# Hybrid trunk on one NeuronCore: the first feed-forward layer in a written order, with the state-space table operations on the vector engine

## The chip, the cores and the metric

The kernel runs on one core of one Trainium2 chip. The time is device microseconds of that core, and the time before is the median of three runs.

## The reference, cut to what matters

A two-layer decoder trunk over 512 positions of 1024 channels. Each layer has a mixer (layer 0: stick-breaking attention beside causal pooling; layer 1: a state-space layer), then a cross-attention into 256 memory tokens, then a gated feed-forward layer. The two parts that the change touches are the feed-forward layer and the constants of the state-space layer:

```python
def conv_gated_mlp(h, w_up, conv_w, conv_b, w_down):     # D_FF = 2816
    up = h @ w_up                                        # 512 x 5632
    padded = jnp.pad(up, ((0, 0), (CONV_WIDTH - 1, 0), (0, 0)))
    conv = conv_b
    for i in range(CONV_WIDTH):                          # 3 taps, causal
        conv = conv + conv_w[i] * padded[:, i:i + seq]
    val, gate = jnp.split(conv, 2, axis=-1)
    return (jax.nn.silu(gate) * val) @ w_down
...
    # s5_ssm: 64 groups of 16 channels, 64 complex states per group
    bb_re = coef_re[..., None] * b_re - coef_im[..., None] * b_im
    bb_im = coef_re[..., None] * b_im + coef_im[..., None] * b_re
    # h_t = Lbar h_{t-1} + Bbar u_t ;  y = Re(C h) + D u
```

The kernel computes the state-space layer in blocks of 8 positions. For that it needs, per group, products of B and of C with powers of Lbar, and a small table of taps made from both. These tables depend on the weights alone. They are made during the first feed-forward layer, written to DRAM, and read back in the state-space layer.

## The kernel before

Everything is held transposed: `xT[m]` are 8 tiles of 128 channels x 512 positions. A projection of 1024 inputs to 128 outputs is 8 steps of `mm3`, and each `mm3` is three matmuls of 512 columns (high x high, high x low, low x high), because every operand is split into two reduced-precision parts. A weight chunk (four 128x128 blocks, 256 KB) is loaded on SP's queue into `wr`, copied by ScalarE to `wh` (L112) and subtracted by VectorE to `wl` (L115). There are four buffers of each, so a chunk can be converted three chunks before the matmuls use it.

The feed-forward layer has 22 hidden blocks in two halves of 11. In a half, each block has an up-projection of the value (`up_conv(j)`) and of the gate (`up_conv(NF + j)`), 24 matmuls each, and then the convolution: a multiply by the norm row on VectorE (L1311), ScalarE's tap (L1313), two taps on VectorE (L1314, L1316). The gate goes through SiLU (L1329), is multiplied (L1330) and split into `hh` and `hl`. Then come 8 down-projections `psd` of 33 matmuls each, added to `xT` by `residual`. This layer appears twice: layer 0 (`ffn` with `side`), and layer 1 with the same work and no side work, to which the first can be compared.

The side work of layer 0 is the generator `ssm_prep`. For 16 blocks of B it forms two products and a sum on GpSimd (L597 to L599, 128x512), which TensorE transposes (`pswi`), ScalarE copies out (L607) and SP writes to `d_win`. For 16 blocks of C it does the same with 9 powers (L643 to L645, 128x576). The result, laid out `[4, 16, 9]`, is copied by ScalarE (L649) and written to `d_wout`; TensorE multiplies it with the B table (`psk`, L654); the taps are copied (L657), get the skip term from two small VectorE operations (L659, L661), are spread by eight small DMAs on SP's queue into `tz` (L665), reordered by ScalarE (L667) and written to `d_t`. All of these transfers are on SP's queue, which also carries every weight chunk.

Most stages of this kernel are under `tc.manual_schedule()`, which keeps the order in which the program is written on each engine. The region of the first feed-forward layer is not: there the framework's planner orders the instructions by its own costs and may move them forward across the region's start. The PSUM banks of that region are split by use (A=2, B=4, C=2). Weight chunks for the two feed-forward layers come from a list of their own (`wcols`, one column block ahead, L123), those of the other stages from one stream `W` (L167), which `take()` keeps three raw chunks and four converted chunks ahead.

The stage before is the first cross-attention, which ends with eight output projections `pso`. GpSimd makes another set of tables there (`ssm_tables`, `d_tab`). The stage behind is the state-space layer. It reads the tables back with GpSimd's queue (`load_x`, `load_y`) and starts with the projections `psu`, then the first use of a table (`psX`, L1513).

Of the kernel before, what the change touches and what calls it, by code (L numbers as in the profile page):

```python
# [52 lines left out]
def trunk_kernel(  # L53
# [21 lines left out]

    pools = {}
# [473 lines left out]
    def ssm_prep(rg):  # L550
        yield
        pB, pBi = (rg.tile([128, 8, 64], F32, tag=f"pw{q}", name="pB") for q in range(2))
        pC, pCi = (rg.tile([128, 9, 64], F32, tag=f"pw{2 + q}", name="pC") for q in range(2))
        for q, t in enumerate((pB, pBi, pC[:, 1:9], pCi[:, 1:9])):
            nc.sync.dma_start(out=t.rearrange("p a b -> p (a b)"), in_=d_pw[q])
# [4 lines left out]
        def raw_pair(src, order, c_major):  # L560
# [4 lines left out]
            d1 = rg.tile([128, 16, 64], F32, tag="rw1", name="rw1")  # L565
            d2 = rg.tile([128, 16, 64], F32, tag="rw2", name="rw2")
            for c0 in (0, 8):
# [4 lines left out]
                o1 = d1[:, c0:c0 + 8, :].rearrange("p a b -> p (a b)")  # L572
                o2 = d2[:, c0:c0 + 8, :].rearrange("p a b -> p (a b)")
                A.activation(out=o1, in_=ps, func=AF.Copy)
                A.activation(out=o2[0:64], in_=ps[64:128], func=AF.Copy)
                A.activation(out=o2[64:128], in_=ps[0:64], func=AF.Copy)
            return d1, d2

        b1, b2 = raw_pair((ssm_b_re[0], ssm_b_im[0]),
                          "g (r p c) -> g r p c", False)  # L580
        yield
        bz = rg.tile([128, 64, 16], F32, tag="bz", name="bz")
        LAG = 4
        pend = []
        for b in range(2 * NB):
            gs = slice(b * 4, b * 4 + 4)
            sh = [128, 4, 16, 8]
            big = rg.tile([128, 4, 16, 8], F32, tag="u2", bufs=9, name="bl")
            bt = rg.tile([128, 4, 16, 8], F32, tag="u2", bufs=9, name="bt")
# [12 lines left out]
            def fin(b=b, big=big):  # L602
                ps = psC("pswi")
                for q in range(4):
                    tr(ps[:, q * 128:(q + 1) * 128], big[:, q].rearrange("p c j -> p (c j)"))
                w = rg.tile([128, 512], F32, tag="ev", bufs=2, name="wi")
                A.activation(out=w, in_=ps, func=AF.Copy)  # L607
                nc.sync.dma_start(out=d_win[b // 2][:, (b % 2) * 512:(b % 2) * 512 + 512], in_=w)

            pend.append(fin)  # L610
            if len(pend) > LAG:
                pend.pop(0)()
            yield

        while pend:
            pend.pop(0)()
            yield
        c1, c2 = raw_pair((ssm_c_re[0], ssm_c_im[0]),
                          "g (c r p) -> g c r p", True)

        dsk = rg.tile([64, 16], F32, tag="dsk", name="dsk")
        nc.sync.dma_start(out=dsk, in_=ssm_d[0].rearrange("(g c) -> g c", c=16))
# [5 lines left out]
        for t in tzs:  # L628
            G.memset(t, 0.0)
# [1081 lines left out]
```

## Time and profile before

| what | value |
|---|---|
| time, median of 3 runs | 1553.75 us (1552.21 to 1555.38) |
| profiled execution, on the device | 1556.48 us |
| its span, first to last instruction | 1554.7 us |
| mean granted TensorE clock | 0.987 |

The profiled execution has 1.8 us around its span and is 2.7 us over the median of the runs. In the rows below, a line such as L115 is a line of the kernel before; a tile name such as `psup` is the program's. PE is TensorE, DVE VectorE, ACT ScalarE, POOL GpSimd, SP the engine that issues most DMAs. A name ending in q is an engine's queue of instructions that are not counted as busy.

### The profile page before, as it was taken

To read this page: it belongs to the slowest core of one execution; us is meant where nothing else is said; L and a number is where in the kernel's file an instruction comes from. 1 tells how busy PE (TensorE), PEld (TensorE's weight loads), DVE (VectorE), ACT (ScalarE), POOL (GpSimd) and SP (SyncE) were. 2 spreads that over 40 slices of the span, in tenths; PEclk is the share of its full clock that TensorE was granted. 3 is DMA by queue.
4 is the path that set the end of the run, shared out by engine and by line. 5 is a ranking of instruction groups with operands and counts; after the bars stand their busy time and mean duration, and the time that the engine had idled before them with its cause. 6 is when DMAs were issued, how large, how long until landed. Compare 5 with 4: busy or idle time off the path is not lost.

```text
span 1554.7 us, 21034 instructions
## 1 busy us (share of the span) xinstructions
PE 1509.6 (97%) x7327; PEld 1238.7 (80%) x7327; DVE 1024.5 (66%) x1523; ACT 727.5 (47%) x1286; POOL 482.2 (31%) x739
## 2 busy tenths in 40 slices
PE   8999999998988999999999999999999999999998
PEld 6787988887866887777778897888888888888887
DVE  4776656665799866887655667455656775367754
ACT  5556664343434542455553546433444443244532
POOL 7775339995399058330000111000000000000002
PEclk9999899999999999999999999999999999999999
DMA  6213234324323533345464877333123333333331
GB/s 193 78 44 105 82 124 124 99 82 136 89 81 95 154 106 108 107 148 181 142 212 139 267 227 243 110 102 89 55 70 101 95 96 92 97 101 96 95 116 54
DMA packets 282613, 183.99 MB, mean 118 GB/s; under 512 B 30279, under 2 KB 260235, under 8 KB 282507
## 3 DMA queue, kind: packets, MB, share of 16 engines
q1 hardware_dynamic: 264011, 149.84, 32.6%
q0 software_dynamic: 7264, 25.20, 4.7%
q10 hardware_dynamic: 11232, 7.61, 1.6%
q8 instruction: 57, 0.93, 0.2%
q14 instruction: 49, 0.40, 0.1%
HBM read 156.13 MB, written 24.12 MB: 116 GB/s over the span
## 4 chain that ended last, share of the span: by engine, by line
PE 70%; POOL 11%; DVE 7%; issue 5%; DMA 3%; ACT 3%; SPq 0%; DVEq 0%; ACTq 0%; POOLq 0%
PE psup L206 8%; PE psup L208 8%; PE psup L207 8%; PE psd L206 5%; PE psd L208 5%; PE psd L207 5%; DVE wl L115 2%; PE psg L206 2%; PE psg L207 2%; PE psg L208 2%; PE pso L207 2%; PE pso L208 2%; PE pso L206 1%; PE psk L654 1%; POOL tb L541 1%
## 5 line engine op out<-in xcount | busy, mean ns | idle before, releaser
L115 DVE TENSOR_TENSOR wl<-wr,wh 128x512 fp32r<-128x512 f32 (+2 forms) x467 | 361.0, 782 | 137.0 <-ACT wh L112 134.7
L112 ACT ACTIVATE wh<-wr 128x512 fp32r<-128x512 f32 (+2 forms) x467 | 283.5, 618 | 318.3 <-PE psd L207 108.3
L208 PE MATMUL psup<-xh,wl 128*128 128x512 f32 x704 | 277.8, 395 | 11.6 <-DVE wl L115 11.6
L206 PE MATMUL psup<-xh,wh 128*128 128x512 f32 x704 | 279.9, 398 | 1.4 <-ACT wh L112 1.4
L207 PE MATMUL psup<-xl,wh 128*128 128x512 f32 x704 | 277.2, 394 | 0.0
L1383 POOL TENSOR_TENSOR acc<-acc,sq 128x256 f32<-128x256 f32 x12 | 8.8, 734 | 559.1 <-ACT sq L1381 558.9
L208 PEld LDWEIGHTS psup<-xh,wl 128*128 128x128 f32 x704 | 133.4, 190 | 44.7 <-DVE wl L115 16.1
L206 PEld LDWEIGHTS psup<-xh,wh 128*128 128x128 f32 x704 | 133.4, 190 | 34.7 <-ACT wh L112 3.5
L207 PEld LDWEIGHTS psup<-xl,wh 128*128 128x128 f32 x704 | 133.5, 190 | 27.5 <-issue 0.5
L206 PE MATMUL psd<-hh,wh 128*128 128x512 f32 x328 | 129.7, 395 | 0.0
L208 PE MATMUL psd<-hh,wl 128*128 128x512 f32 x328 | 129.1, 394 | 0.0
L207 PE MATMUL psd<-hl,wh 128*128 128x512 f32 x328 | 129.0, 393 | 0.0
L1313 ACT ACTIVATE fc<-fu,ccols 128x512 f32<-128x512 f32 x88 | 71.8, 816 | 103.1 <-DVE fu L1311 103.1
L1314 DVE SCALAR_TENSOR_TENSOR fc<-fu,ccols,fc 128x511 f32<-128x511 f32 x88 | 71.7, 814 | 24.0 <-ACT fc L1313 24.0
L1311 DVE TENSOR_TENSOR fu<-psup,rbc 128x512 f32<-128x512 f32 x88 | 60.3, 685 | 40.2 <-PE psup L208 37.6
L1316 DVE SCALAR_TENSOR_TENSOR fc<-fu,ccols,fc 128x510 f32<-128x510 f32 x88 | 75.3, 856 | 2.9
L206 PEld LDWEIGHTS psd<-hh,wh 128*128 128x128 f32 x328 | 61.6, 188 | 16.3 <-issue 1.3
L208 PEld LDWEIGHTS psd<-hh,wl 128*128 128x128 f32 x328 | 61.6, 188 | 14.3
L207 PEld LDWEIGHTS psd<-hl,wh 128*128 128x128 f32 x328 | 61.6, 188 | 14.0
L301 ACT ACTIVATE xh<-xT,gcols 128x512 fp32r<-128x512 f32 x40 | 33.5, 838 | 83.3 <-DVE xT L324 55.0
L206 PE MATMUL pso<-oh,wh 128*128 128x512 f32 x128 | 51.1, 399 | 4.9 <-ACT wh L112 4.9
L115 DVE TENSOR_TENSOR hl<-fc,hh 128x512 fp32r<-128x512 f32 x44 | 37.3, 847 | 25.8 <-ACT hh L112 25.6
(331 smaller groups left out, 3388.0 us busy)
## 6 DMA issues: line engine op xcount, KB each, us to landing
wr<-in_ffn_w_up_dram SPq DMA_DIRECT2D x176, 256.0 KB, 2.9
wr<-in_ffn_w_down_dram SPq DMA_DIRECT2D x70, 256.0 KB, 2.9
wr<-in_xa_w_kv_dram SPq DMA_DIRECT2D x64, 256.0 KB, 3.3
wr<-in_ab_w_in_dram SPq DMA_DIRECT2D x32, 256.0 KB, 2.9
wr<-in_xa_w_q_dram SPq DMA_DIRECT2D x32, 256.0 KB, 2.8
wr<-in_xa_w_o_dram SPq DMA_DIRECT2D x32, 256.0 KB, 2.8
wr<-in_ssm_w_glu_dram SPq DMA_DIRECT2D x29, 256.0 KB, 2.7
wr<-in_ffn_w_down_dram SPq DMA_DIRECT2D x24, 192.0 KB, 2.6
```

The lines of the kernel that those rows point to most:

```text
L112: A.activation(out=o, in_=i, func=AF.Copy)
L115: V.tensor_tensor(out=o, in0=i, in1=hi.bitcast(F32), op=ALU.subtract)
L206: T.matmul(ps, lhsT=lh, rhs=rh, start=first, stop=False)
L207: T.matmul(ps, lhsT=lh, rhs=rl, start=False, stop=False)
L208: T.matmul(ps, lhsT=ll, rhs=rh, start=False, stop=last)
L301: A.activation(out=ho, in_=src, func=AF.Copy, scale=g)
L541: G.tensor_tensor(out=dst[0], in0=dst[0], in1=tq[:, :, :c], op=ALU.subtract)
L654: T.matmul(ps[0:16, q * 128:(q + 1) * 128], lhsT=bz[:, b * 4 + q, :], rhs=big[:, q, :, 0:8].rearrange("p c m -> p m c"), start=True, stop= ...
L1311: V.tensor_tensor(out=u, in0=ps, in1=rbc, op=ALU.mult)
L1313: A.activation(out=c, in_=u, func=AF.Identity, scale=cwcol(layer, 2, t), bias=cbcol(layer, t))
L1314: V.scalar_tensor_tensor(out=c[:, 1:], in0=u[:, :511], scalar=cwcol(layer, 1, t), in1=c[:, 1:], op0=ALU.mult, op1=ALU.add)
L1316: V.scalar_tensor_tensor(out=c[:, 2:], in0=u[:, :510], scalar=cwcol(layer, 0, t), in1=c[:, 2:], op0=ALU.mult, op1=ALU.add)
```

## The change

The first feed-forward layer gets a function of its own, `ffn_side`, under `manual_schedule` and with all eight PSUM banks in one pool. Its weights come from the stream `W`, whose list now runs unbroken from the cross-attention through this layer and the state-space layer. The gate product and its split are written one convolution later. The generator of the side work is stepped by hand: once in each convolution, and in the down-projections 2, 2 and 1 times behind the chunks of the first half and once behind each chunk of the second. A step issues one table operation, and what follows from it is issued a fixed number of steps later (`at(n, f)`).

The products and sums of the tables move from GpSimd to VectorE. The C table is laid out `[4, 9, 16]`, so `psk` reads 128 contiguous columns, while ScalarE's copy of it is now the one with a stride. The two small tap operations move from VectorE to GpSimd, and the copy of B's last power to ScalarE. All loads and stores of the side work move from SP's queue to GpSimd's. At the start of the kernel eight matmuls on a tile of ones are added and the first value step is split in two.

```diff
+    np_.tile([128, 32], F32, tag="pad", name="pad")
...
-                nc.sync.dma_start(out=rv[:, :, q, :] if c_major else rv[:, q], in_=src[q])
+                nc.gpsimd.dma_start(out=rv[:, :, q, :] if c_major else rv[:, q], in_=src[q])
...
-            G.tensor_tensor(out=big, in0=vb(b1), in1=vp(pB), op=ALU.mult)
-            G.tensor_tensor(out=bt, in0=vb(b2), in1=vp(pBi), op=ALU.mult)
-            G.tensor_tensor(out=big, in0=big, in1=bt, op=ALU.add)
-            G.tensor_copy(bz[:, gs, :], big[:, :, :, 7])
+            V.tensor_tensor(out=big, in0=vb(b1), in1=vp(pB), op=ALU.mult)
+            yield
+            V.tensor_tensor(out=bt, in0=vb(b2), in1=vp(pBi), op=ALU.mult)
+            yield
+            V.tensor_tensor(out=big, in0=big, in1=bt, op=ALU.add)
...
+            at(2, turn)
+            at(3, keep)
+            at(4, put)
...
-            sh = [128, 4, 16, 9]
+            sh = [128, 4, 9, 16]
...
-                    T.matmul(ps[0:16, q * 128:(q + 1) * 128], lhsT=bz[:, b * 4 + q, :],
-                             rhs=big[:, q, :, 0:8].rearrange("p c m -> p m c"), start=True, stop=True)
+                    T.matmul(st["ps"][0:16, q * 128:(q + 1) * 128], lhsT=bz[:, b * 4 + q, :],
+                             rhs=big[:, q, 0:8, :], start=True, stop=True)
...
-                V.tensor_tensor(out=kt[:, :, 0, :], in0=kt[:, :, 0, :], in1=dd, op=ALU.add)
+                G.tensor_tensor(out=kt[:, :, 0, :], in0=kt[:, :, 0, :], in1=dd, op=ALU.add)
...
-                    nc.sync.dma_start(out=tz[j:128:8, :, j * 16:128], in_=ktf[:, :, 0:128 - j * 16])
+                    nc.gpsimd.dma_start(out=tzs[b % 2][j:128:8, :, j * 16:128], in_=ktf[:, :, 0:128 - j * 16])
...
+            for n, f in ((1, wout), (2, taps), (2, put_wout), (3, keep), (3, spread), (8, band), (9, put_band)):
+                at(n, f)
...
+    ffn_weights(0)
+    ssm_weights()
+    xattn_weights(1)
...
+        warm = psC("warm")
+        for _ in range(8):
+            T.matmul(warm[:, 0:128], lhsT=ones, rhs=ones, start=True, stop=True)
         W.cap[0] = 1
         x_tile(0)
         W.fill()
+        v_step(0, range(2))
         x_tile(1)
         W.cap[0] = 2
         W.fill()
-        v_step(0)
+        v_step(0, range(2, 4))
...
+    def ffn_side(rg, layer, norm, hid_extra, nxt, side):
+        acts = norm.acts
+        SIDE = ((2, 2, 1), (1, 1, 1))
+        st = {"n": 0}
+        wait = {}
+        def conv(t, ps):
+            u = rg.tile([128, 512], F32, tag="fu", bufs=2, name="fu")
+            V.tensor_tensor(out=u, in0=ps, in1=st["rbc"], op=ALU.mult)
+            c = rg.tile([128, 512], F32, tag="fc", bufs=3, name="fc")
+            A.activation(out=c, in_=u, func=AF.Identity, scale=cwcol(layer, 2, t), bias=cbcol(layer, t))
+            gate = wait.pop("gate", None)
+            if gate:
+                cv, cg, hl = gate
+                V.tensor_tensor(out=cv, in0=cv, in1=cg, op=ALU.mult)
+                copy_hi(hl[0], cv)
+            next(side, None)
+            V.scalar_tensor_tensor(out=c[:, 1:], in0=u[:, :511], scalar=cwcol(layer, 1, t), in1=c[:, 1:],
+                                   op0=ALU.mult, op1=ALU.add)
+            V.scalar_tensor_tensor(out=c[:, 2:], in0=u[:, :510], scalar=cwcol(layer, 0, t), in1=c[:, 2:],
+                                   op0=ALU.mult, op1=ALU.add)
+            if gate:
+                sub_lo(hl[1], cv, hl[0])
+            return c
...
+                for n in SIDE[hf]:
+                    hi, lo = W.take()
...
+                    for q in range(hi.shape[1]):
+                        mm3(ps, hi[:, q, :], lo[:, q, :], hid[k][0], hid[k][1], k == 0, k == NH - 1)
+                        k += 1
+                    for _ in range(n):
+                        next(side, None)
+                residual(m, ps)
...
-    with banks(A=2, B=4, C=2), region("rgB") as rg:
+    with banks(X=8), region("rgB") as rg, tc.manual_schedule():
         side = ssm_prep(rg)
-        ffn(rg, 0, n_f0, 4, n_mix1, side)
+        next(side)
+        ffn_side(rg, 0, n_f0, 4, n_mix1, side)
```

## Rows read from the trace of the kernel before

**Rows 1.** Page, part 1: busy time, share of the span, instructions.

```profile
PE 1509.6 (97%) x7327; PEld 1238.7 (80%) x7327; DVE 1024.5 (66%) x1523; ACT 727.5 (47%) x1286; POOL 482.2 (31%) x739
```

**Rows 2.** Windows: stretch, length, busy time of PE, PEld, DVE, ACT, POOL; clock; DMA.

```profile
380.00:396.15 16.15, 16.10 (x60) 13.06 (x61) 11.03 (x17) 7.82 (x13) 0.00 (x0) 0.84 0.48 137
396.15:549.46 153.31, 140.94 (x615) 111.30 (x614) 132.28 (x143) 67.33 (x111) 93.65 (x64) 0.96 0.36 105
549.46:616.67 67.21, 67.11 (x303) 52.27 (x301) 42.49 (x43) 23.64 (x40) 54.80 (x31) 1.00 0.35 104
616.67:761.29 144.62, 144.04 (x617) 107.00 (x616) 109.18 (x151) 76.02 (x119) 30.71 (x23) 1.00 0.48 144
761.29:828.22 66.93, 66.93 (x290) 51.91 (x290) 34.68 (x51) 34.88 (x50) 3.73 (x7) 1.00 0.60 189
828.22:853.63 25.41, 25.41 (x124) 20.94 (x122) 15.43 (x35) 9.89 (x18) 1.82 (x2) 1.00 0.42 127
1177.15:1298.86 121.71, 121.71 (x540) 100.29 (x539) 90.20 (x143) 59.34 (x90) 0.00 (x0) 1.00 0.32 94
1298.86:1360.45 61.59, 61.59 (x266) 49.55 (x264) 23.26 (x36) 16.52 (x28) 0.00 (x0) 1.00 0.33 97
1360.45:1480.14 119.69, 119.69 (x529) 99.10 (x528) 87.57 (x129) 57.45 (x87) 0.00 (x0) 1.00 0.34 99
```

**Rows 3.** Waits, 416 to 549.46 us: total us, times, longest.

```profile
PE psup L208 <- DVE wl L115: 11.0, 8, 2.1
```

**Rows 4.** Groups by line, DVE, 416 to 549.46 us: busy, mean ns | idle before.

```profile
L115 DVE TENSOR_TENSOR wl<-wr,wh 128x512 fp32r<-128x512 f32 x38 | 44.5, 1171 | 0.3 <-ACT wh L112 0.3
```

**Rows 5.** Groups by line, DVE, 1360.45 to 1480.14 us (the second feed-forward layer).

```profile
L115 DVE TENSOR_TENSOR wl<-wr,wh 128x512 fp32r<-128x512 f32 x44 | 30.2, 686 | 2.1 <-ACT wh L112 1.9
```

**Rows 6.** Groups by line, POOL, whole span.

```profile
L598 POOL TENSOR_TENSOR bt<-rw,pB 128x512 f32<-128x512 f32 x16 | 30.2, 1884 | 0.0
```

**Rows 7.** Waits of SP's queue, 270 to 860 us.

```profile
SPq L564 <- DMA d_tab<-tb: 17.5, 1, 17.5
```

**Rows 8.** Timeline of SP, 373 to 376 us: start, length, instruction.

```profile
375.33 1.07 SPq L167 DMA_DIRECT2D wr<-in_xa_w_o_dram  x2
```

**Rows 9.** Timeline of PE at 380 us; in brackets the idle time before and its releaser.

```profile
380.05 0.80 PE L206 MATMUL pso<-oh,wh 128*128 128x512 f32 x1 [4.92 <-ACT wh L112]
```

**Rows 10.** Timeline of PE, 597 to 600 us: one group of tap matmuls.

```profile
597.29 2.00 PE L654 MATMUL psk<-dl,bz 128*16 128x128 f32 x8
599.22 0.50 PE L206 MATMUL psd<-hh,wh 128*128 128x512 f32 x1
```

**Rows 11.** Timeline of PE, 549.4 to 550.2 us: one group of transposes.

```profile
549.46 0.60 PE L216 MATMUL pswi<-cs,bl 128*128 128x128 f32 x4
549.82 0.48 PE L206 MATMUL psd<-hh,wh 128*128 128x512 f32 x1
```

**Rows 12.** Groups by line, DVE, whole span: an operand read with a 32-byte stride.

```profile
L1639 DVE TENSOR_TENSOR xT<-xT,sig 128x512 f32<-128x512 f32 x8 | 9.3, 1168 | 0.2
```

**Rows 13.** Instructions of L548: issue time on POOL, ns min/median/max, first and last start.

```profile
L548 POOL DMA_DIRECT2D d_tab<-tb x16: 551/568/667, 243.7 to 370.5; - x16
```

**Rows 14.** Instructions of tile tz: issue time on SP; then from issue to landing.

```profile
L665 SPq DMA_DIRECT2D tz<-kt x128: 544/593/1493, 600.6 to 799.0; - x128
...
DMA to landing us min/median/max: 1.7/1.9/8.6
```

**Rows 15.** Timeline of POOL, 600 to 850 us: table reads of the state-space layer.

```profile
788.05 0.54 POOL L1490 DMA_DIRECT2D wo<-d_wout  x1 [1.78 <-ACT wo L649]
844.99 0.92 POOL L1505 DMA_DIRECT2D sg<-d_u  x1 [56.40 <-DMA d_u<-su]
```

**Rows 16.** DMA issues by line: count, KB each, median us to landing.

```profile
wo<-d_wout POOLq DMA_DIRECT2D x8, 512.0 KB, 7.3
```

**Rows 17.** Timeline of DVE, 12 to 13 us: the second converted weight chunk.

```profile
12.22 0.69 DVE L115 TENSOR_TENSOR wl<-wr,wh 128x512 fp32r<-128x512 f32 x1 [1.69 <-ACT wh L112]
```

**Rows 18.** Timeline of PE, 12 to 14.2 us: the first matmul that uses that chunk.

```profile
13.91 0.48 PE L206 MATMUL psv<-wh,xh 128*128 128x512 f32 x1
```

More of the change, by code (lines that the diff above doesn't have):

```diff
@@ L610, in ssm_prep @@
-            pend.append(fin)
-            if len(pend) > LAG:
-                pend.pop(0)()
-            yield
[L615 to L622, printed above, removed]
-        ps = psC("psds")
-        tr(ps[0:16, 0:64], dsk, 64)
-        dcol = rg.tile([16, 64], F32, tag="dcol", name="dcol")
@@ L1286, in xattn, with ffn @@
             nxt.tile(m)
-    def ffn(rg, layer, norm, hid_extra, nxt, side=None, tail=0):
+    def ffn(rg, layer, norm, hid_extra, tail):
         acts = norm.acts
@@ L1325, in ffn @@
                 cv = up_conv(j)
-                if pace[0] != "slow":
-                    pace[0] = next(side, None)
                 cg = up_conv(NF + j)
@@ L1339, in ffn @@
                 sub_lo(hl[1], cv, hl[0])
-                pace[0] = next(side, None)
                 hid.append(hl)
@@ L1354, in ffn, with up @@
                     late.append(hl)
-                pace[0] = next(side, None)
                 residual(m, ps)
-                if hf == 1 and not tail:
+        finish(hid[NH - tail:], late)
+    def ffn_side(rg, layer, norm, hid_extra, nxt, side):
[21 more added lines that the diff above has]
+            return c
+        def up(t):
+            ps = psB("psup")
+            sproj(ps, acts)
+            if "rc" not in st:
+                st["rc"] = norm.stats_cols()
+                st["first"] = ps
+                return None
+            if "rbc" not in st:
+                st["rbc"] = norm_row(st["rc"], 4)
+            return ps
+        for hf in range(2):
+            hid = []
+            for j in range(hf * NH, (hf + 1) * NH):
+                ps = up(j)
+                cv = conv(j, ps) if ps is not None else None
+                ps = up(NF + j)
+                if cv is None:
+                    cv = conv(j, st.pop("first"))
+                cg = conv(NF + j, ps)
+                A.activation(out=cg, in_=cg, func=AF.Silu)
+                hl = []
+                for nm in ("hh", "hl"):
+                    if st["n"] % 12 < hid_extra:
+                        hl.append(rg.tile([128, 512], F32R, tag="hx", bufs=2 * hid_extra, name=nm))
+                    else:
+                        hl.append(ttile(nm))
+                st["n"] += 1
+                hid.append(hl)
+                wait["gate"] = (cv, cg, hl)
+            for m in range(KD):
+                ps = psA("psd")
+                k = 0
+                for n in SIDE[hf]:
+                    hi, lo = W.take()
+                    gate = wait.pop("gate", None)
+                    if gate:
+                        cv, cg, hl = gate
+                        V.tensor_tensor(out=cv, in0=cv, in1=cg, op=ALU.mult)
+                        copy_hi(hl[0], cv)
+                        sub_lo(hl[1], cv, hl[0])
+                    for q in range(hi.shape[1]):
[4 more added lines that the diff above has]
+                residual(m, ps)
+                if hf == 1:
```

212 lines of the change are left out of this document (127 added, 85 removed).

## The prediction

> **What bounds the kernel now.** The page's busy times come first. TensorE is busy for 97% of the span, VectorE for 66%, ScalarE for 47% and GpSimd for 31% [rows 1]. So time can only be won where TensorE waits, where it runs at half clock, or where it does something that it need not. Busy time alone shows none of the three, because a stretched matmul counts as busy.
>
> The second view is the windows, one for each half and part of the two feed-forward layers [rows 2]. The second layer does the same 1584 matmuls of projection without side work, so its stretches are the measure: 121.71 us for the first 22 up tiles, 119.69 for the other 22, 61.59 for eight down tiles. Its last down part has another form, so 61.59 stands for both. The sum is 121.71 + 61.59 + 119.69 + 61.59 = 364.6 us. The first layer takes 153.31 + 67.21 + 144.62 + 66.93 = 432.1 us. The excess is 67.5 us.
>
> Next, what fills that excess. The side work's own matmuls are seen in the timeline. A group of eight tap matmuls takes 599.22 - 597.29 = 1.93 us [rows 10], and there are 16 groups, 30.9 us. A group of four transposes `pswi` takes 549.82 - 549.46 = 0.36 us [rows 11], 16 groups are 5.8 us. The other side transposes (`psrw`, `psds`), 33 in number, are some 3 us at the same 0.09 each. That is 39.7 us, and 67.5 - 39.7 = 27.8 us remain that are no work at all.
>
> Most of the 27.8 us lies in the first up part: 153.31 - 121.71 - 6.8 (15 groups `pswi` and 16 of the other transposes) = 24.8. There VectorE is busy 132.28 of 153.31 us, and GpSimd 93.65 [rows 2]. The waits name the link: matmuls of `psup` stand waiting for `wl`, the low half of a weight chunk from VectorE, 11.0 us in 8 waits [rows 3], and the clock of the stretch is 0.96 [rows 2]. The groups by line show why `wl` is late: it takes 1171 ns here [rows 4] and 686 ns in the second layer [rows 5]. The difference between the two stretches is that GpSimd's table operations, 1884 ns each [rows 6], run beside VectorE's in the first. In the other parts VectorE has less to do and the slower operations stay hidden.
>
> Last, the cross-attention's end. SP's queue holds the side work's first load (L564), moved forward by the planner, and it waits 17.5 us for `d_tab` [rows 7]. The next weights stand behind it and are issued at 375.33 [rows 8]. [...]
>
> **The change part by part.**
>
> *Table products off GpSimd.* With them goes what slows VectorE. I take the 27.8 us of lost time in the first layer as gone, provided that VectorE can carry the work itself. That is 96 operations in 96 steps, 64 products and 32 sums. A sum is contiguous, 0.69 us [rows 5], and 0.77 for 576 columns in proportion. A product reads one operand with a stride of 256 bytes. The trace has no such operation on VectorE; below, it can't be cheaper than contiguous, 0.69; the nearest row above is an operand at 32 bytes, 1.17 [rows 12]; the far bound is GpSimd's 1.88 [rows 6]. I take 1.17, and 1.3 for 576 columns, since stride is what the row has in common. A step is then 1.01 us (B) or 1.12 (C) on average.
>
> An up part takes 22 steps, 22 to 25 us, on top of 87.57 to 90.20: 112 of some 126 us. The first down part takes 40 steps (8 tiles x 5), 42 us, on top of 23.26: 65 us. TensorE's side there is 61.59 + 10 x 0.36 and about two tap groups, 66 to 67 us. The second takes 16 table operations, 18 us, and the eight norm tiles of some 1.9 us (one strided, one contiguous operation), so 23.26 + 18 + 15 = 56 of 66 us. So VectorE stays below TensorE everywhere, closest in the first down part. Being late by a few us there is covered: conversion runs three chunks ahead, and a chunk of 12 matmuls is 12 x 119.69/528 = 2.7 us, so 8 us of cover. Term: -27.8 us; the bounds are -27.8 and, with products at 1.88, -17 (below).
>
> *The tap matmuls read contiguous columns.* Now 128 columns take 1.93/8 = 0.241 us each, with the elements 36 bytes apart. In the same kernel, 128 contiguous columns of a transpose take 0.36/4 = 0.09 [rows 11], and a 512-column matmul 0.227, so 0.057 for 128. If stride is not the reason, 0.241 stays. I take 0.09, the row of the same width and type: 128 x (0.241 - 0.09) = -19.3 us, with bounds 0 and 128 x (0.241 - 0.057) = -23.6. [...]
>
> *Side transfers off SP's queue.* The load that blocked weights now waits on GpSimd's queue, behind the same `d_tab` stores, where only the table work waits for it; its first use is the third step, behind two up tiles. So the 4.92 us go, and with them the slow clock, 16.15 x 0.16 = 2.6 us. Term: -7.5 us; bound 0, if another load is late there.
>
> On GpSimd a DMA issue takes 0.57 us [rows 13], against SP's 0.59 for `tz` [rows 14]. A C block issues two stores and eight small DMAs and has two operations of 64 columns, which I put at 0.45 each, twice an eighth of [rows 6]'s 1.88: some 6.6 us of GpSimd. Blocks come every 16 us in the up part, every 5 in the first down part (three blocks), every 7.5 in the second. The chain that matters is the single buffer `kt`: ScalarE copies taps, then 0.9 + 8 x 0.57 + 1.9 to landing [rows 14] = 7.4 us until it may copy again. In the first down part ScalarE stands for some 2 us once; behind it the next weight conversions wait, and the 8 us of cover hold. At nothing, then, and at the price of the rival below if the chain is longer.
>
> *What moves to a later point.* Before, the state-space layer's first table reads were issued during the feed-forward layer, the tenth at 788.05 [rows 15], 40 us before the layer began. Now GpSimd's queue keeps program order, and all ten (512 KB each) are issued in the first 10 x 0.54 = 5.4 us of that layer, behind the last `put_band`. Each lands in 7.3 us [rows 16]. The first two are wanted with `psX` 25.4 us after the start, which covers them. What is late next is `sg(0)`, issued 16.8 us after the start (844.99 - 828.22) [rows 15], behind them in the same queue. It has 25.41 - 16.8 = 8.6 us until `psX` and needs some 7.3, so it fits if its own source, written in the same traffic, isn't late. Bounds 0 and +8 us (one more landing); I take +2.
>
> *At nothing:* the eight matmuls on ones run while TensorE waits for the first input; the split value step only moves matmuls before the second chunk, which is ready at 12.91 [rows 17], and first used at 13.91 [rows 18], so up to 1 us either way. ScalarE's strided copies: it has half of its time free [rows 2]. The late gate product has a whole convolution before its first use.
>
> Sum: -27.8 - 19.3 - 7.5 + 2 = -52.6 us. For the profiled execution, 1556.48 - 52.6 = 1503.9 (span 1554.7 plus 1.8); it was 2.7 over the median, so against the median 1553.75 - 52.6 = 1501.
>
> **The rivals.**
>
> *VectorE becomes the bound.* If a stride of 256 bytes costs 1.88 per product, the first down part has 23.26 + 27 x 1.88 + 13 x 0.7 = 83 us of VectorE against 66, 17 us late, of which the cover of conversions ahead takes some 6: 11 us. Elsewhere it still fits. 1501 + 11 = 1512. For it: no row has that stride. Against: stride costs the same 2 ns for an element on VectorE (1.17/512) and TensorE (0.241/128 = 1.9).
>
> *The layout is not why the taps are slow.* They stay at 0.241, and the time is 1501 + 19 = 1520. For it: their weights are only 16 columns wide, which no other row has.
>
> *The state-space layer waits for its tables.* The reads and `sg(0)` land 8 to 12 us late: about 1510. For it: ten reads, weights and `d_u` at once. Against: the projections hold more than 25 us.
>
> *The spread of the taps on GpSimd's queue becomes the pace, and the kernel is slower.* ScalarE stands still for every block whose chain is longer than the distance of blocks. Some 7.6 blocks are at 7 us, the rest at 16. From a chain of 7 + 53/7.6 = 14 us the whole gain is gone; at 16 us it is 7.6 x 9 = 68 us, 1569 us. [...] Against: the stores of `d_tab` took 0.67 us at most beside a working VectorE [rows 13], and the eight need not land one after another.
>
> **How the numbers follow.** The forecast has 0.62, VectorE as the bound 0.10, slow taps 0.08, late tables 0.12, the slow chain 0.04; 0.04 is left for what I don't see. The forecast's own range is 1495 (taps at 0.057, no wait at the tables, 4 + 2 us) to 1509. 1494 to 1522 holds the first four but for their edges, and I go to 1492 and 1523 for the 1.6 us by which the runs shown lie around their median. A change of 0.2%, 3 us, is what a measurement of this kernel tells from none. Faster by more: 0.94. Within: 0.02. Slower: 0.04.
>
> **What would show it.** In the changed profile the first feed-forward layer takes about 385 us, with parts near 127, 67, 128 and 64. `wl` has a mean near 0.69 throughout. A group of eight tap matmuls takes 0.7 us. TensorE's idle time at the cross-attention's end is gone. Products on VectorE are near 1.17 and 1.3 us. GpSimd's reads are issued at the state-space layer's start, and `psX` follows some 25 to 28 us after it. The prediction is wrong if ScalarE is seen waiting for `tz`'s DMAs by many us at a time, or if `wl` stays late with GpSimd idle.

## The result and the profile after

| what | before | after |
|---|---|---|
| median of 4 runs each, side by side | 1552.98 us (1551.05 to 1555.38) | 1514.44 us (1513.06 to 1515.88) |
| ratio, with its 95% interval | | 0.9751 [0.9733, 0.9769] |
| profiled execution | 1556.48 us | 1513.59 us |
| its span | 1554.7 us | 1511.8 us |

The change makes the kernel 38.5 us faster. The forecast was 52.6 us faster, 1501 us. The two profiled spans differ by 42.9 us, because the profiled execution of before lay 3.5 us above the median beside it and that of after 0.9 below: the shares below are of the 42.9.

The windows of the kernel after, by stage: the four parts of the first feed-forward layer, the head of the state-space layer in two pieces, and three parts of the second feed-forward layer. Columns as in [rows 2].

```profile
387.45:515.83 128.38, 128.38 (x593) 105.04 (x591) 102.26 (x160) 64.79 (x110) 3.90 (x6) 1.00 0.36 102
515.83:586.56 70.73, 68.24 (x325) 54.95 (x324) 58.86 (x77) 27.72 (x55) 12.77 (x26) 1.00 0.46 141
586.56:715.71 129.15, 129.15 (x594) 103.94 (x592) 107.37 (x153) 70.63 (x108) 47.20 (x94) 1.00 0.43 127
715.71:783.72 68.01, 68.01 (x313) 53.45 (x313) 50.80 (x66) 46.28 (x63) 41.44 (x85) 1.00 0.51 159
783.72:810.21 26.49, 25.58 (x124) 20.80 (x122) 12.61 (x29) 8.31 (x15) 6.91 (x15) 1.00 1.00 344
810.21:830.00 19.79, 16.30 (x89) 14.75 (x90) 14.13 (x22) 9.65 (x18) 4.44 (x7) 0.74 0.65 211
1137.23:1258.94 121.71, 121.71 (x539) 100.30 (x538) 90.26 (x143) 59.34 (x90) 0.00 (x0) 1.00 0.33 94
1258.94:1318.78 59.84, 59.84 (x266) 49.55 (x264) 23.18 (x36) 16.41 (x28) 0.00 (x0) 1.00 0.34 99
1318.78:1438.46 119.68, 119.68 (x530) 99.10 (x528) 87.75 (x129) 57.36 (x87) 0.00 (x0) 1.00 0.34 99
```

The first layer takes 128.38 + 70.73 + 129.15 + 68.01 = 396.27 us, against 432.07 in [rows 2] and 385 in the forecast. TensorE is now busy all through three of its four parts, and the clock is 1.00 in all four. Two things in this table differ from the forecast: the head of the state-space layer, where the transfer engines are at 1.00 and the clock then falls to 0.74, and the second layer's down part, 59.84 us for the same work that took 61.59 [rows 2]. The stretch ahead of the layer, the cross-attention's end, has no idle time and full clock now:

```profile
353.00:387.45 34.45, 34.45 (x153) 28.54 (x152) 23.33 (x33) 15.21 (x26) 21.12 (x43) 1.00 0.54 153
```

VectorE's groups by line in the first up part (416 to 515.8 us): `wl`, a multiply that reads PSUM, and a product of the tables.

```profile
L116 DVE TENSOR_TENSOR wl<-wr,wh 128x512 fp32r<-128x512 f32 x37 | 23.9, 687 | 12.8 <-ACT wh L113 12.8
...
L1451 DVE TENSOR_TENSOR fu<-psup,rbc 128x512 f32<-128x512 f32 x18 | 12.3, 685 | 0.0
L640 DVE TENSOR_TENSOR bl<-rw,pB 128x512 f32<-128x512 f32 x6 | 6.9, 1145 | 0.0
```

`wl` is back at 687 ns [rows 4, 5], and a product takes 1.14 us where 1.17 was taken. Next, TensorE's timeline: a group of tap matmuls, and the one wait in the layer.

```profile
592.09 1.05 PE L700 MATMUL psk<-dl,bz 128*16 128x128 f32 x8
593.07 0.50 PE L207 MATMUL psup<-xh,wh 128*128 128x512 f32 x1
593.41 0.40 PE L208 MATMUL psup<-xl,wh 128*128 128x512 f32 x1
```

```profile
526.69 0.66 PE L217 MATMUL pswi<-cs,bl 128*128 128x128 f32 x4 [2.49 <-DVE bl L644]
```

The group takes 593.07 - 592.09 = 0.98 us, 0.122 for each of its eight records, against 0.241 [rows 10] and the 0.09 of the forecast. The program writes four matmuls for a group and the trace has eight records, two for each. The 2.49 us are all of TensorE's idle time in the first down part: transposes asked for a sum that VectorE had not reached.

Last, the head of the state-space layer, in TensorE's timeline and in GpSimd's.

```profile
810.21 1.97 PE L1668 MATMUL psX<-sg,wi 128*128 128x64 f32 x16 [0.91 <-DMA sg<-d_u]
815.66 3.65 PE L1668 MATMUL psX<-sg,wi 128*128 128x64 f32 x16 [3.49 <-DMA sg<-d_u]
```

```profile
784.45 0.55 POOL L1636 DMA_DIRECT2D wi<-d_win  x1
...
794.04 0.54 POOL L1645 DMA_DIRECT2D wo<-d_wout  x1 [2.11 <-DMA tb<-d_tab]
804.98 0.92 POOL L1660 DMA_DIRECT2D sg<-d_u  x1 [10.41 <-DMA d_u<-su]
```

Eight of the ten reads are issued in the first 5 us; the last two wait 2.68 and 2.11 us for earlier reads and go at 791.39 and 794.04, where the forecast had all ten within 5.4 us. `sg` is late at both `psX`, and from 814 to 822 us, in and behind the second wait, the clock is 0.50. It is not late by its place in GpSimd's queue: the queue stands 10.41 us waiting for `d_u`, the store that `sg` reads back, which is on ScalarE's queue. That store before and after, issues up to 860 us:

```profile
L1501 ACTq DMA_DIRECT2D d_u<-su x3: 326/333/333, 842.4 to 851.5; - x3
...
DMA to landing us min/median/max: 2.0/3.3/4.6
```

```profile
L1656 ACTq DMA_DIRECT2D d_u<-su x6: 326/329/333, 798.0 to 845.7; - x6
...
DMA to landing us min/median/max: 2.0/5.6/6.5
```

It is first issued 14.2 us after the stage's start before and 14.3 after. But `sg` can follow 844.99 - 842.4 = 2.6 us later before [rows 15] and 804.98 - 798.0 = 7.0 us later now, in the stretch whose transfer engines are at 1.00.

### The profile page after: what moved, and what is told of

It is laid out like the page before. It is cut to its first block, busy times and chain, and to the rows that moved or that the text cites. A ratio compares the mean times of both kernels' runs of the same rounds, so it can differ in the third digit from the quotient of the medians.

```text
span 1511.8 us, 21035 instructions
## 1 busy us (share of the span) xinstructions
PE 1484.0 (98%) x7343; PEld 1236.9 (82%) x7343; DVE 1024.2 (68%) x1586; ACT 734.4 (49%) x1303; POOL 414.2 (27%) x844
## 4 chain that ended last, share of the span: by engine, by line
PE 89%; issue 3%; DMA 2%; DVE 2%; POOL 2%; ACT 1%; POOLq 0%; DVEq 0%; ACTq 0%
PE psup L207 11%; PE psup L209 11%; PE psup L208 11%; PE psd L207 5%; PE psd L209 5%; PE psd L208 5%; PE pso L208 2%; PE pso L209 2%; PE pso L207 2%; PE psg L207 2%; PE psg L209 2%; PE psg L208 2%; PE psq L207 2%; PE psq L209 2%; PE psq L208 2%
## 5 line engine op out<-in xcount | busy, mean ns | idle before, releaser
L116 DVE TENSOR_TENSOR wl<-wr,wh 128x512 fp32r<-128x512 f32 (+2 forms) x467 | 324.1, 710 | 137.6 <-ACT wh L113 136.8
L207 PE MATMUL psup<-xh,wh 128*128 128x512 f32 x704 | 275.9, 392 | 0.0
L209 PE MATMUL psup<-xh,wl 128*128 128x512 f32 x704 | 274.1, 389 | 0.0
L1453 ACT ACTIVATE fc<-fu,ccols 128x512 f32<-128x512 f32 x44 | 36.0, 817 | 92.9 <-DVE fu L1451 92.9
L207 PEld LDWEIGHTS psd<-hh,wh 128*128 128x128 f32 x328 | 61.6, 188 | 14.3 <-issue 1.7
L209 PEld LDWEIGHTS psd<-hh,wl 128*128 128x128 f32 x328 | 61.6, 188 | 13.4
L715 POOL DMA_DIRECT2D tz<-kt x128 | 65.1, 516 | 7.4 <-POOL kt L712 4.7
L303 DVE SCALAR_TENSOR_TENSOR xl<-xT,gcols,xh 128x512 fp32r<-128x512 f32 x40 | 35.1, 878 | 34.2 <-ACT xh L302 34.0
L658 POOL DMA_DIRECT2D d_win<-wi x16 | 8.7, 544 | 154.9 <-ACT wi L655 154.9
L207 PE MATMUL psq<-xh,wh 128*128 128x512 f32 x128 | 51.1, 399 | 0.0
L1398 DVE TENSOR_TENSOR fu<-psup,rbc 128x512 f32<-128x512 f32 x44 | 30.3, 688 | 29.1 <-PE psup L209 27.7
```

Of the source, the lines that this page charges most:

```text
L116: V.tensor_tensor(out=o, in0=i, in1=hi.bitcast(F32), op=ALU.subtract)
L207: T.matmul(ps, lhsT=lh, rhs=rh, start=first, stop=False)
L209: T.matmul(ps, lhsT=ll, rhs=rh, start=False, stop=last)
L303: V.scalar_tensor_tensor(out=lo, in0=src, scalar=g, in1=ho.bitcast(F32), op0=ALU.mult, op1=ALU.subtract)
L658: nc.gpsimd.dma_start(out=d_win[b // 2][:, (b % 2) * 512:(b % 2) * 512 + 512], in_=st["w"])
L715: nc.gpsimd.dma_start(out=tzs[b % 2][j:128:8, :, j * 16:128], in_=ktf[:, :, 0:128 - j * 16])
```

## The experiments

Ratios are to the kernel before, run beside each.

### Tables back on GpSimd, everything else new

```diff
-            V.tensor_tensor(out=big, in0=vb(b1), in1=vp(pB), op=ALU.mult)
+            G.tensor_tensor(out=big, in0=vb(b1), in1=vp(pB), op=ALU.mult)
```

(and the same for the other five lines of products and sums)

> The kernel after with one part undone: the 96 table operations (64 products, 32 sums) are issued on GpSimd again, in the new fixed order, with the new layout and with the transfers still on GpSimd's queue. My theory: GpSimd's table operations slow VectorE's. Then wl goes back from 0.72 us on average to about 1.17 in the first feed-forward layer, matmuls of psup wait for it again, and most of the 27.8 us come back: 1535 to 1545 us. Above that if GpSimd itself, with 40 steps of up to 1.9 us and its transfers in the first down part, falls behind its 70 us. Rival: the planner's order and SP's queue had made the chunks late, not the engine. Then wl may be slow but little waits: 1512 to 1518 us.

Measured: 1555.71 us, ratio 1.0 [0.9988, 1.0012]. The whole gain is gone, more than the 20 to 30 us that the theory's 1535 to 1545 us stand for. The layer takes 439.6 us. The waits say why it is too much: TensorE's in the layer (total us, times, longest), and one of ScalarE's from 598 us on.

```profile
PE psup L209 <- DVE wl L116: 7.7, 4, 2.8
PE psk L700 <- POOL dl L681: 7.1, 4, 2.9
```

```profile
ACT kt L705 <- DMA tz<-kt: 15.0, 6, 6.2
```

Beside the late `wl`, GpSimd itself is late with tables (`dl`), and ScalarE waits 15.0 us for the spread of the taps: the chain that the prediction's slower rival named does occur when GpSimd carries tables and transfers at once. Two costs stand in one number, so the next two runs part them. What the written order is worth by itself was not run: no kernel here has the tables on VectorE under the planner.

### Tables on GpSimd, stores and spread on SP; and all transfers on SP with tables on VectorE

```diff
+            G.tensor_tensor(out=big, in0=vb(b1), in1=vp(pB), op=ALU.mult)
...
+                nc.sync.dma_start(out=d_win[b // 2][:, (b % 2) * 512:(b % 2) * 512 + 512], in_=st["w"])
```

(the same for all six lines of products and sums, and for the other stores and the spread; the two small tap operations go to VectorE, and the loads stay on GpSimd's queue)

> The kernel after with the 96 table operations on GpSimd, as in the run before with that edit, but with the stores and the eight small spreading transfers of each block back on SP's queue and the two small operations of the spread back on VectorE; the loads stay on GpSimd's queue. That run gave the layer 439.6 us, and two costs stood in it together: VectorE's operations slowed by GpSimd's, and GpSimd's queue, which carried tables and transfers at once (15.0 us of waits for tz, 7.1 for dl). Theory: the first of the two is the one that the prediction priced at 27.8 us; without the second the layer then takes 396 + 20 to 28 = 416 to 424 us and the time is 1536 to 1545 us. Rival: the overloaded queue is all of it, and slower operations on VectorE cost little in the new order; then the layer is back at 398 to 403 us and the time at 1516 to 1522 us.

```diff
-                nc.gpsimd.dma_start(out=rv[:, :, q, :] if c_major else rv[:, q], in_=src[q])
+                nc.sync.dma_start(out=rv[:, :, q, :] if c_major else rv[:, q], in_=src[q])
```

(and so for every load, store and spread of the side work)

> The kernel after with one part undone: all of the side work's transfers, loads, stores and spread, are on SP's queue again; the fixed order, the layout and the tables on VectorE stay. Theory: in program order the side work's first load, which waits for d_tab, stands ahead of the weights on SP as it did before, so the 4.9 us of idle time and the slow clock come back (7.5 us), and the stores behind evictions hold up weights now and then: 1521 to 1530 us. Rival: the new order puts the loads late enough, or weights early enough, that SP's queue would have done as well: 1512 to 1517 us.

Measured: 1550.87 us, ratio 0.9961 [0.9941, 0.9981], and 1528.28 us, ratio 0.9817 [0.979, 0.9843]. The first is above what was expected. SP's queue has a price too (10.2 us in the layer, below), so the run to hold it against is the second, whose stores and spread are also on SP. Windows of the layer's parts, tables on GpSimd and then on VectorE:

```profile
386.96:534.37 147.41, 135.24 (x593) 107.03 (x591) 112.28 (x141) 64.95 (x110) 43.04 (x27) 0.95 0.32 89
534.37:607.01 72.64, 69.93 (x325) 56.30 (x324) 43.33 (x41) 26.71 (x53) 64.93 (x40) 0.98 0.41 126
607.01:744.06 137.05, 134.81 (x593) 102.31 (x592) 96.92 (x142) 71.19 (x108) 40.56 (x24) 1.00 0.41 120
744.06:818.66 74.60, 71.03 (x313) 54.78 (x313) 44.48 (x65) 46.04 (x64) 14.27 (x9) 0.95 0.49 144
```

```profile
385.95:514.36 128.41, 128.41 (x593) 105.05 (x591) 102.31 (x160) 64.76 (x110) 0.28 (x1) 1.00 0.36 102
514.36:585.04 70.68, 68.19 (x325) 54.98 (x324) 58.82 (x77) 26.97 (x53) 1.62 (x2) 1.00 0.44 133
585.04:715.96 130.92, 129.95 (x594) 103.70 (x592) 104.19 (x147) 70.98 (x108) 8.03 (x16) 1.00 0.42 122
715.96:792.39 76.43, 71.53 (x313) 55.07 (x313) 52.56 (x69) 45.86 (x64) 10.73 (x14) 0.96 0.49 142
```

431.70 against 406.44 us: the tables on GpSimd cost 25.3 us, 19.0 of them in the first up part, and by the ratios (0.9961 - 0.9817) x 1556 = 22.4. The two runs also differ in the loads' queue and in the engine of the two small tap operations. In the first up part neither counts: no tap operation runs yet, and the kernel after, with its loads on GpSimd's queue, takes 128.38 us there against the 128.41. VectorE is busy 112.28 us in that part without the tables and 102.31 with them, because its own operations take longer beside GpSimd's. How much of the price falls there depends on where the table operations lie: in the run before this pair, 19 of them lie in that part in place of 25, and it takes 136.68 us. The marks of that in the first run, 416 to 534 us:

```profile
L116 DVE TENSOR_TENSOR wl<-wr,wh 128x512 fp32r<-128x512 f32 x35 | 31.1, 928 | 11.9 <-ACT wh L113 11.9
...
L1451 DVE TENSOR_TENSOR fu<-psup,rbc 128x512 f32<-128x512 f32 x18 | 12.3, 682 | 0.0
```

`wl`, with two inputs in SBUF, goes from 687 to 928 ns on average; `fu`, which reads one input from PSUM, stays at 682, against 685. The other operations with two inputs in SBUF (both taps, the gate product, `hl`) take 859 to 1192 ns in this run and 683 to 751 in the kernel after. In the kernel before, from 416 to 549.46 us, they take 1049 to 1383 and `fu` 680. Why the two kinds differ was not tried.

The second run differs from the kernel after by the queues alone: +10.2 us in the layer, 8.4 of them in its last part. SP's queue stood 24.7 us for `kt` and 16.3 for `wi` in all. From 700 to 800 us TensorE waits 2.5 us for `hh` and 2.4 for `dl`, and the clock is 0.96 in the last part. Its time fell in the expected range, but not for the first reason given. The layer starts at 385.95, no later than with GpSimd's queue, and the load that was to wait doesn't; instructions of that line on SP, start in us:

```profile
L578 SPq DMA_DIRECT2D raw<-in_ssm_b_re_dram x1: 591/591/591, 345.3 to 345.3; - x1
```

It is issued while GpSimd still writes `d_tab` (until 368 us), so in the new kernel it does not wait for them. Whether the order or the tile's new place in SBUF freed it was not tried.

### The kernel before, its loads alone on GpSimd's queue

```diff
-                nc.sync.dma_start(out=rv[:, :, q, :] if c_major else rv[:, q], in_=src[q])
+                nc.gpsimd.dma_start(out=rv[:, :, q, :] if c_major else rv[:, q], in_=src[q])
```

> The kernel before with one part of the change alone: the four loads of the power tables and the loads of the raw B and C tables go from SP's queue to GpSimd's; all else is as before, the planner included. Theory: the load that waits for d_tab on SP's queue holds up the weights behind it; without it TensorE's 4.92 us of idle time at the cross-attention's end and the slow clock behind it go: 1553 - 7.5 = 1545 to 1546 us. Rival: the planner puts another load there, or GpSimd's queue now stands for 17 us with the table operations behind it and the layer pays that back: 1550 to 1556 us.

Measured: 1548.37 us, ratio 0.9966 [0.9947, 0.9986], 5.3 us faster [2.2, 8.2]; the expected 7.5 lies within. The profile is of the fastest of ten runs, 1543.5 us. The last 32 us of the cross-attention:

```profile
355.00:386.85 31.85, 31.85 (x142) 26.36 (x141) 21.01 (x31) 15.01 (x26) 18.27 (x34) 1.00 0.62 149
```

TensorE has no idle time and full clock; the layer starts at 386.85 and not at 396.15 [rows 2], 9.3 us earlier, and itself takes 432.8 us, as before. So the load on SP's queue was the cause of that loss in the kernel before. Either half of the change removes it alone: the loads' queue here, everything else in the run before this one.

### The tap tables strided again

```diff
-            return rg.tile([128, 4, 9, 16], F32, tag="u2", bufs=5, name=name)
+            return rg.tile([128, 4, 16, 9], F32, tag="u2", bufs=5, name=name)
...
-                             rhs=big[:, q, 0:8, :], start=True, stop=True)
+                             rhs=big[:, q, :, 0:8].rearrange("p c m -> p m c"), start=True, stop=True)
```

> The kernel after with one part undone: the C tables have the old layout again, so the 128 tap matmuls read elements 36 bytes apart; engines, order and queues stay new. Theory: the stride is what made them slow. They go from 0.122 to 0.241 us each, and since TensorE is busy all through the layer the time grows by 128 x 0.119 = 15.2 us, to 1529 to 1531 us. Rival: the narrow weights (16 columns) or the pairing of two float32 passes set the pace and the layout only moved the work. Then they stay near 0.12 and the time stays within 1512 to 1517 us.

Measured: 1531.56 us, ratio 0.9849 [0.9824, 0.9874], 0.0098 above the kernel after's, some 15 us with about 5 us of uncertainty, because the two ratios come from separate measurements. The profiled layer takes 413.22 us, 16.95 more than the kernel after's, 3.45 of it in the first down part, whose clock is 0.98 and whose two groups of taps account for 1.9. One group in TensorE's timeline:

```profile
577.93 2.00 PE L700 MATMUL psk<-dl,bz 128*16 128x128 f32 x8
579.86 0.50 PE L207 MATMUL psd<-hh,wh 128*128 128x512 f32 x1
```

1.93 us again, as in [rows 10]. Stride was the reason, and by the records the term is 128 x (0.241 - 0.122) = 15.2 us.

### Without the products; without the side work's matmuls

The first kernel leaves out the 96 table operations; its tables are two tiles filled with a constant.

```diff
-            V.tensor_tensor(out=big, in0=vb(c1), in1=vp(pC), op=ALU.mult)
             yield
-            V.tensor_tensor(out=bt, in0=vb(c2), in1=vp(pCi), op=ALU.mult)
             yield
-            V.tensor_tensor(out=big, in0=big, in1=bt, op=ALU.add)
```

> The kernel after without its 96 table operations: the products and sums are left out, and the transposes, tap matmuls, copies and transfers use two tiles that are filled once. It asks whether VectorE is why the layer takes 396.3 us and not the forecast 385.1. Theory A: VectorE sets only the one wait of 2.5 us at the first down part; the rest is TensorE's own (tap matmuls at 0.122, and the first wide matmul behind each narrow group 0.1 us longer). Then the layer takes 393 to 394 us, and the time is 1511 to 1513 us. Theory B: VectorE's load makes the chunks late all through. Then the layer comes near 385 to 387 us and the time is 1503 to 1506 us.

Measured: 1510.2 us, ratio 0.9718 [0.9697, 0.9739]. Two of the layer's windows:

```profile
515.77:583.54 67.77, 67.77 (x325) 55.09 (x324) 22.46 (x35) 27.69 (x56) 12.87 (x26) 1.00 0.47 147
583.54:712.69 129.15, 129.15 (x594) 103.91 (x592) 87.67 (x130) 70.34 (x109) 47.19 (x93) 1.00 0.43 127
```

The layer takes 393.15 us. The first down part loses its wait (70.73 to 67.77), and the second up part takes 129.15 us with 87.67 us of VectorE as with 107.37. The layer is where theory A has it, and the time 0.8 us under A's range: VectorE costs one wait, and the rest is TensorE's own.

The second kernel leaves out the transposes `pswi` and the tap matmuls; ScalarE copies the tables themselves.

```diff
-                    tr(st["ps"][:, q * 128:(q + 1) * 128], big[:, q].rearrange("p c j -> p (c j)"))
...
-                    T.matmul(st["ps"][0:16, q * 128:(q + 1) * 128], lhsT=bz[:, b * 4 + q, :],
-                             rhs=big[:, q, 0:8, :], start=True, stop=True)
```

> The kernel after without the 64 transposes of the B tables and the 128 tap matmuls: ScalarE copies from the tables themselves instead, so that its work and the transfers stay. It sizes what the prediction counted as lost time. The groups left out take 16 x 0.36 + 16 x 0.98 = 21.4 us. Theory: each group also costs the first wide matmul behind it 0.1 us, 3.2 us in all, so that the layer takes 396.3 - 24.6 = 371.7 us, and some 2.5 less if the wait at the first down part is gone with its transposes: 1486 to 1491 us. Rival: the 0.1 us are only how the records are drawn; then the layer takes 374 to 375 us and the time is 1492 to 1494 us.

Measured: 1496.81 us, ratio 0.961 [0.959, 0.9629]. The layer's four windows:

```profile
389.04:515.02 125.98, 125.98 (x573) 103.06 (x571) 99.93 (x156) 64.51 (x110) 3.91 (x6) 1.00 0.36 104
515.02:580.14 65.12, 62.69 (x265) 50.64 (x264) 60.74 (x80) 27.57 (x54) 13.10 (x25) 0.97 0.49 149
580.14:700.06 119.92, 119.92 (x530) 98.95 (x528) 102.41 (x146) 69.40 (x106) 46.27 (x89) 1.00 0.45 135
700.06:769.49 69.43, 63.81 (x265) 49.84 (x264) 55.18 (x73) 48.45 (x68) 48.61 (x90) 0.98 0.52 159
```

380.45 us, neither of the two numbers expected, and the time is above both ranges: in the down parts TensorE now waits 5.2 us for `hh` and the clock falls to 0.97 and 0.98, so that the last one is longer than in the kernel after (69.43 against 68.01). The up parts answer the question. The second goes from 129.15 to 119.92, 9.23 us for eight groups of 0.98, so 0.17 us a group beyond its own time; the first from 128.38 to 125.98, 2.40 us for five groups of 0.36, so 0.12 a group. For 16 groups of either kind that is 4.6 us. The timeline shows where it lies: matmuls of 512 columns start every 0.227 us, but the one behind a group of taps takes 593.41 - 593.07 = 0.34 us until the next starts, as it does in the kernel before, and the one ahead of it 0.32. And 119.92 is near the second layer's 119.69 [rows 2]: in that part VectorE carries the tables at next to no cost.

### Without the unused 128 bytes

```diff
-    np_.tile([128, 32], F32, tag="pad", name="pad")
```

> The kernel after without the line that reserves 128 bytes per partition at the head of SBUF and is never used. The second feed-forward layer's down parts, which the change does not touch otherwise, went from 61.59 to 59.84 us and from 48.0 to 46.75 us. Theory: the 128 bytes shift every tile behind them and with that where the down tiles' operands lie; without them the pitch of psd goes back from 0.2267 to 0.2333 us and the time grows by 3.0 us, 1516 to 1519 us. Rival: the other changes of the tiles' sizes moved the addresses, or it is no matter of addresses: the stretches stay 59.84 and 46.75 us and the time within 1513 to 1516 us.

Measured: 1516.7 us, ratio 0.9744 [0.9718, 0.977], too wide to tell 3 us. The window of the second layer's first down part tells it:

```profile
1256.63:1318.22 61.59, 61.59 (x265) 49.58 (x264) 23.17 (x36) 16.40 (x28) 0.00 (x0) 1.00 0.33 96
```

61.59 us again, to the digit of [rows 2]: the line that the prediction did not price is worth 1.75 us here. That the 1.25 us of the last down part (48.00 to 46.75) come from the same line is an estimate. Which tile's place matters stays open.

### The state-space layer's reads later

```diff
-            seq(lx(0), lx(1), lx(2), ly(0), ly(1), kvm.load, um(0), st, um(1), row, uo(0), sg(0), ac(0), um(2), uo(1), sg(1), ac(1), ac(2), uo(2), ac(3), um(3), sg(2))
+            seq(lx(0), kvm.load, um(0), st, um(1), row, uo(0), sg(0), lx(1), ac(0), um(2), uo(1), sg(1), ac(1), ac(2), ly(0), lx(2), uo(2), ac(3), um(3), sg(2), ly(1))
```

> The kernel after with another order of GpSimd's queue at the state-space layer's start: only the first block's table reads stand ahead of sg(0); the second's go behind it, and those of the third block and both blocks' wq and wo behind sg(1). Nothing else changes. Theory: the ten reads of 512 KB keep the transfer engines at a share of 1.00 until past 810 us, so that d_u and sg come late, TensorE waits 0.91 and 3.49 us at the first two psX, and the clock falls for 10 us behind them. With four reads fewer ahead, both waits and the slow stretch go: 5 to 8 us, 1506 to 1510 us. Rival: psX is late by the chain through d_u itself, or wq and wo now come late for psY: the wait only moves, and the time stays within 1512 to 1517 us.

Measured: 1511.53 us, ratio 0.971 [0.9684, 0.9737], in neither expected range: 3 us faster than the kernel after by the medians, 6 by the ratios, and the intervals overlap. From the first `psu` to the first `psg` the layer takes 144.91 us, against 150.47 in the kernel after. The first wait is gone, the second is still there:

```profile
815.08 2.77 PE L1668 MATMUL psX<-sg,wi 128*128 128x64 f32 x16 [2.92 <-issue]
```

The view names no releaser for it. This order had put two reads of 512 KB between `sg(0)` and `sg(1)`, and `sg(1)` is issued at 810.58, behind 7.22 us of waiting for its `d_u`. The last version puts both `sg` behind four reads and ahead of the rest, and makes the transposes one step later.

```diff
+            seq(lx(0), lx(1), kvm.load, um(0), st, um(1), row, uo(0), sg(0), ac(0), um(2), uo(1), sg(1), ac(1), ac(2), ly(0), lx(2), uo(2), ac(3), um(3), sg(2), ly(1))
...
-            at(2, turn)
-            at(3, keep)
-            at(4, put)
+            at(3, turn)
+            at(4, keep)
+            at(5, put)
```

> The kernel after with two edits that the earlier runs point to. First, GpSimd's queue at the state-space layer's start: the four table reads of the first two blocks, then sg(0) and sg(1), and only then wq, wo and the third block's reads (the earlier try had put the second block's reads between sg(0) and sg(1), and the second psX still waited 2.92 us). Second, the transposes of a B block one step later, with its copy and its store, so that the first down part does not wait 2.5 us for a sum of VectorE. Theory: the first down part takes 67 to 68.5 us in place of 70.7, both psX come without a wait and no stretch at half clock follows them; together 8 to 11 us against the kernel after, 1503 to 1507 us. Rival: the late transposes only move the wait to another block, and psX waits for d_u in any order; then 1509 to 1514 us.

> The kernel after, unchanged, beside the version above on one chip, so that the two are compared under the same conditions: 1513 to 1517 us, a ratio of 0.973 to 0.977 to the kernel before.

Measured, side by side: 1508.18 us, ratio 0.9694 [0.9675, 0.9714], and 1514.43 us, ratio 0.9721 [0.9701, 0.9741]. That is 6.3 us by the medians and 4.2 by the ratios, less than the 8 to 11 expected, and the intervals still overlap. The unchanged kernel's ratio was 0.9751 before and is 0.9721 here, so ratios of separate measurements agree to some 0.003. The windows show where it lies: the first down part and the state-space layer up to `psg`, of the new version and then of the kernel after again.

```profile
516.09:586.33 70.24, 68.73 (x328) 54.96 (x326) 59.65 (x78) 27.38 (x55) 12.61 (x25) 1.00 0.45 142
783.49:808.91 25.42, 25.42 (x124) 20.95 (x123) 14.26 (x33) 9.64 (x18) 5.89 (x13) 1.00 0.78 253
808.91:928.30 119.39, 113.57 (x769) 103.10 (x768) 82.63 (x123) 62.05 (x105) 22.81 (x39) 0.99 0.84 269
```

```profile
515.80:589.36 73.56, 71.06 (x326) 57.10 (x324) 58.93 (x77) 27.54 (x55) 12.79 (x25) 0.95 0.44 136
786.52:937.22 150.70, 142.15 (x891) 126.90 (x890) 97.40 (x155) 71.97 (x122) 28.75 (x51) 0.95 0.81 256
```

`psX` comes 25.42 us after the start, as in the kernel before [rows 2], and the stage takes 25.42 + 119.39 = 144.81 in place of 150.70. The second `psX` still waits 0.79 us, and from 813 to 817 us the clock is 0.57, so a slow stretch is still there. The late transposes helped only in part: 1.1 us of the wait stay.

## Why the prediction came out 13 us from its point

The sign, the range and the mechanisms held; three sizes were off, and one line was not priced. The forecast of -52.6 us is 14.1 from the medians' -38.5 (13.4 in the time itself, because the median before moved from 1553.75 to 1552.98): 9.7 us to the profiled spans' -42.9, and 4.4 from there by which executions were profiled. In us of the profiled spans:

| term | forecast | measured | by |
|---|---|---|---|
| lost time in the layer | -27.8 | -20.6 | 432.07 - 396.27, less the taps' 15.2 |
| tap matmuls | -19.3 | -15.2 | 0.122 each; the strided run: 15.2 |
| cross-attention's end | -7.5 | -7.6 | distance of the two traces before and behind it |
| state-space layer's tables | +2 | +4.6 | 150.47 - 145.85, first `psu` to first `psg` |
| second layer's down parts | 0 | -3.0 | 61.59 - 59.84 = 1.75, the run without the 128 bytes; 48.00 - 46.75 = 1.25, the two traces |
| start of the kernel, slow clock near 161 us in the trace before | 0 | -1.0 | the two traces; from 160 to 162 us clock 0.50 before, 0.88 after |
| sum | -52.6 | -42.8 | spans: -42.9 |

The last two terms, 4.0 us that the prediction had at nothing, fell in the forecast's direction by luck; without them the sum is -38.8.

*Lost time.* The cause is shown: the two runs that differ in the tables' engine are 25.3 us apart in the layer, 19.0 of them in a part where nothing else that differs counts. The step that failed is the remainder: 67.5 us of excess less the side matmuls' own 39.7 was called no work at all. But 4.6 of the 27.8 us are what narrow groups cost the wide matmuls beside them, in both kernels, and 2.5 us came back as the first down part's wait: 27.8 - 4.6 - 2.5 = 20.7. VectorE was said to be closest to TensorE in just that part (65 of 66 to 67 us; it was busy 58.86 of 70.73), and the cover of conversions ahead was counted on; but what was late was a sum for the transposes, and no chunk ahead covers that.

*Taps.* The reason was right, the size was not: a record of a tap matmul takes 0.122 us where a transpose of the same width takes 0.09, and the program's one matmul is two such records. Whether the 16 columns of weights or the two records make the difference was not tried. The prediction's bound of 0.057, a wide matmul's time in proportion, is further off than the transpose's 0.09.

*Cross-attention's end.* The size is right: 4.92 us of idle time [rows 9], and behind it a clock of 0.50 from 380.05 to 384 us in the kernel before, 0.84 on average up to 396.15 [rows 2]. The reason, SP's queue, is shown for the kernel before, and was not needed in the new one.

*State-space head.* What was named as late next, `sg(0)`, is late, and `sg(1)` more so: 0.91 and 3.49 us of waits and 8 us at clock 0.50. The prediction's condition is what failed, that its source isn't late: `d_u`, written in the same traffic, holds `sg` back 7.0 us in place of 2.6. The +4.6 us are within the 0 to 8 given, near its middle.

*The other rivals.* VectorE is not the bound: products take 1.13 to 1.23 us. The slow chain does not occur in this kernel; the spread's transfers land as in this answer for line L715:

```profile
L715 POOL DMA_DIRECT2D tz<-kt x128: 508/511/552, 579.3 to 776.7; - x128
...
DMA to landing us min/median/max: 1.6/2.5/4.8
```

## What to carry to other kernels

Take an operation off an engine that slows a neighbour before asking whether the new engine is faster: here moving 96 operations to a busier engine gave TensorE 20.6 us back, and that engine's own load cost one wait of 2.5. When a difference between two stages is split into work and lost time, price what a piece of work does to its neighbours before calling the remainder lost. When reads move to another point in time, look at every transfer that is under way beside them, on other queues too: ten reads of 512 KB ahead of a store and its reload cost 4.6 us, and with six of the ten placed behind, the stage took 144.81 us, against 145.85 before the change.

## What was not expected of the hardware

- A tile of 128 bytes per partition that nobody uses, at the head of SBUF, changed 264 matmuls of another stage from 61.59/264 = 0.233 us to 59.84/264 = 0.227 each, and without it they were back at 61.59.
- A group of narrow matmuls costs TensorE more than its own time: 0.12 us for four transposes and 0.17 for eight records of taps, as the run without them shows. It lies in the wide matmuls beside the group, 0.32 and 0.34 us in place of 0.227 for a group of taps.
- The same wait of 2.5 us goes with a lower clock in one execution and not in another: the first down part took 73.56 us at a mean clock of 0.95 in the one and 70.73 at 1.00 in the other.
